# Rows parted by even and odd in a triangular inverse, element-wise work moved from GpSimd to VectorE, and gates one chunk ahead

## The chip, the cores and the metric

The kernel runs on one core of one Trainium2 chip. The metric is device time in microseconds (us) of one execution. The engines are TensorE (PE), VectorE (DVE), ScalarE (ACT), GpSimd (POOL) and SyncE (SP, which issues the DMAs here).

## The reference, cut to what matters

A first block (stick-breaking attention, cross-attention to a memory, a convolutional feed-forward) is followed by a second block, and the change touches the second alone. On 512 tokens of width 1024 it computes:

```python
h = rms_norm(x, pre_norm_w)
p = h @ w_in
p_rwkv, p_conv, p_pool, p_gate = split(p)
y_a = rwkv7_branch(...)    # 8 heads of 64; a linear recurrence over the 512 tokens
y_b = short_conv_branch(...)     # b * conv(c * u) * silu(z)
y_c = pool_branch(...)           # windows of 2, 4, 8, 16, mixed, * silu(z)
proj = einsum('nbsc,ncd->nbsd', stack([y_a, y_b, y_c]), w_branch)
gates = sigmoid(p_gate.reshape(b, s, 3, 1024))
merged = einsum('bsnd,nbsd->bsd', gates, proj)
out = x + rms_norm(merged @ w_out, post_norm_w)
```

The recurrence is computed in chunks of 64 tokens. Each chunk needs the inverse of a unit lower triangular 64x64 matrix, which is put together from the inverses of its two 32x32 diagonal blocks.

## The kernel before, in words

**Products and weights.** Everything is float32. A product is three passes of TensorE over a high and a low part of each operand (`mm3`: hi·hi, hi·lo, lo·hi). Weights come in units of 512 KB: SP loads `wr`, ACT casts it to `wh` (L135), and an engine subtracts for the low part `wl` (L136); which engine is what `lo_ring[0]` names, DVE as a rule, and GpSimd (`G`) while the inverse runs. Two units can be loaded ahead, four converted. A chunk is one unit's product with the whole input: 24 matmuls of 512 columns, into one of three PSUM banks of tag "g". The bank is free when DVE or ACT has read it. A product of a branch (`ps_br`) is 12 matmuls in a bank of the same three.

**Order.** Each engine runs its instructions in the order in which the program writes them. The program writes the chunks of the second block one after another: RWKV inputs, short convolution (`short_conv(i)`: four chunks each, read by `cu`, `cy`, `cz_s`), `merge(1)`, RWKV inputs, `pool(i)`, z chunks and `merge(2)`, gate chunks, `merge(0)`. Between them, `tick()`, once for about eight matmuls of 512 columns, moves generators on that run in the background. The table `WAIT` says for how many ticks each step of a generator waits. The RWKV branch is such a generator: `rwkv_steps(b)`, for b = 0 and 1, each for two of the four pairs of heads. Its first run lies beside `short_conv` and `merge(1)`, called the first stage here, its second beside the z chunks and `merge(2)`, the second stage.

**The inverse.** In `rwkv_steps` the 64 blocks of 32x32 lie in `ab`, one on each of 64 partitions. For j from 0 to 30, DVE multiplies a row of the block by a column of what is inverted so far (`tm`, L1142, (j+1)(31-j) elements a partition) and adds it to the rows not yet done (`xt`, L1144). After two values of j the generator yields for a tick. Then `xt` goes by a DMA to DRAM (`xtd`, L1151), comes back in another layout by four (`xc`, L1153), waits `WAIT["xc"]` ticks, is transposed on DVE (`xn`, L1157), and is multiplied on TensorE (`ps_x`, L1164), with the rest of the chunk solve, the states and the outputs behind it.

**The merges.** `merge(n)` goes through eight output slices d. For each it computes a gate chunk and its sigmoid (ACT, `gate`), then the branch product `ps_br` from the split branch output (`yb` for n = 1, `yp` for n = 2, L227 the high part on ACT, L228 the low part on GpSimd), and multiplies and adds on DVE and GpSimd (L1368 to L1371). Before the first `ps_br` the program ticks until all four parts of the branch output are split.

Of the kernel before, what the change touches and what calls it, by code (L numbers as in the profile page):

```python
# [10 lines left out]
F32 = mybir.dt.float32  # L11
# [39 lines left out]
class Split:  # L51
# [7 lines left out]
WAIT = {  # L59
# [5 lines left out]
}  # L65
# [3 lines left out]
def model_kernel(ctx: ExitStack, tc: tile.TileContext, a: dict, out: bass.AP, dbg: dict):  # L69
    nc = tc.nc  # L70
    stop = dbg.get("stop")
    V, G, A, T = nc.vector, nc.gpsimd, nc.scalar, nc.tensor
# [23 lines left out]
    def sub(s, *idx):  # L96
        return Split(s.hi[idx], s.lo[idx])
# [8 lines left out]
    ahead, lo_ring = [3], [V]  # L106
# [210 lines left out]
    for f0, f1 in parts:  # L317
# [6 lines left out]
        else:  # L324
# [1 line left out]
    units += [a["w_in"][16]]  # L326
    units += [a["w_in"][4 * n + p] for p in (0, 1) for n in range(3)]
    units += [a["w_in"][c + i] for i in range(4) for c in (21, 25, 17, 29)]
    merge_units = lambda n: [u for d in range(0, 8, 2)
                             for u in (a["w_in"][41 + 8 * n + d], a["w_br"][n, d // 2], a["w_in"][42 + 8 * n + d])]  # L330
    units += merge_units(1)
    units += [a["w_in"][4 * n + p] for p in (2, 3) for n in range(3)]
    units += [a["w_in"][c + i] for i in POOLS for c in (33, 37)]
# [209 lines left out]
    for hp in range(NPAIR):  # L543
# [6 lines left out]
        if hp:  # L550
            q = gemm_q()
            k = gemm_k()
        else:
# [6 lines left out]
            q, k = gemm_q(pss[0]), gemm_k(pss[1])  # L560
# [19 lines left out]
    for c in range(KC):  # L580
        ps = chunk(memT, M)
# [146 lines left out]
    for n in range(2):  # L728
# [7 lines left out]
        for m in range(2):  # L736
            d = (ALLS, m, slice(n * 512, (n + 1) * 512))
# [56 lines left out]
    for c in range(KC):  # L794
        ps = chunk(hT)
# [38 lines left out]
    x2 = dram.tile([NT, P, D], F32, name="x2")  # L834
# [33 lines left out]
    for pi, (f0, f1) in enumerate(parts):  # L868
        if pi:
            run_ahead(spare_in(bigt("wxh", [P, 8, 512]), bigt("wxl", [P, 8, 512])))  # L870
        for f in range(f0, f1):
# [3 lines left out]
            for isv in range(2):  # L875
                ps = lead.pop(0)() if lead else chunk(hT)
# [70 lines left out]
    b2 = ctx.enter_context(tc.tile_pool(name="b2", bufs=1))  # L947
# [4 lines left out]
    def temp(name, shape=None, dt=F32):  # L952
        return b2.tile(shape or [P, S], dt, tag="e", bufs=6, name=name)
# [4 lines left out]
    def quad(name, shape, dt=F32):  # L958
        return b2.tile(shape, dt, tag="q4", bufs=3, name=name)
# [25 lines left out]
    def silu(x, name, ps=False, make=temp):  # L985
        sg = make(name + "_s")
        A.activation(sg, x, AF.Sigmoid)
        (V if ps else G).tensor_tensor(sg, x, sg, ALU.mult)
        return sg

    NB2 = 2
# [6 lines left out]
    ycur, zss, ysplit, normed = {}, {}, set(), set()  # L998
# [7 lines left out]
    def rwkv_pair(p, ab, abd, a21):  # L1006

        r, k, v = rkv.pop(p)
        q = p % NB2
        sg, ai = slot("sg"), slot("ai")  # L1010
        for z, (o, b) in enumerate(((sg, "w0"), (ai, "a0"))):
            ps = bank("b", "ps_wa")
# [7 lines left out]
        ps = bank("b", "ps_ss")  # L1020
# [16 lines left out]
        ps = bank("b", "ps_ri")  # L1037
# [11 lines left out]
        ps = bank("b", "ps_rk")  # L1049
# [24 lines left out]
        ps = tokens(v)  # L1074
# [14 lines left out]
        for e in range(2):  # L1089
            for h in range(2):  # L1090
# [1 line left out]
                    nc.sync.dma_start(abd[q, e, :, h, c].rearrange("t j i -> j t i"),  # L1092
                                      aa[e][rows(2 * (1 - h) + c), h::2, 32 * c:32 * c + 32])
                nc.sync.dma_start(a21[rows(2 * h), q, 4 * e:4 * e + 4], aa[e][rows(2 * (1 - h)), h::2, 32:64])
        q0 = 32 * q
        nc.sync.dma_start(ab[q0:q0 + 32], abd[q].rearrange("e t h c j i -> (e t h c) j i"))
        yield wait["ac"]
        at_ = slot("at", [P, NT, P])
        A.copy(at_, tokens(ar[:, q, 0]))
# [2 lines left out]
        for h in range(2):  # L1102
            ps = tokens(kbh.rearrange("p t z i -> p (t z i)")[:, 512 * h:512 * h + 512])
# [3 lines left out]
        ps = bank("c", "ps_av", [P, NT, 2, CH])  # L1107
# [9 lines left out]
    def rwkv_steps(b):  # L1117

        pairs = (2 * b, 2 * b + 1)
        ab = quad("ab", [64, 32, 32])  # L1120
        abd = dram.tile([NB2, 2, NT, 2, 2, 32, 32], F32, name=f"abd{b}")
        xtd = dram.tile([NB2, 2, NT, 4, 32, 32], F32, name=f"xtd{b}")
        a21 = slot("a21", [P, NB2, 8, 32])
# [7 lines left out]

        yield from together(*[prepared(p) for p in pairs])

        xt = quad("xt", [64, 32, 32])
        G.memset(xt, 0.0)
        G.memset(xt.rearrange("p j i -> p (j i)")[:, 0::33], 1.0)
        yield
        lo_ring[0] = G
        for j in range(31):
            n = 31 - j  # L1140
            tm = b2.tile([64, 256], F32, tag="tm", bufs=1, name="tm")[:, 0:(j + 1) * n].rearrange("p (c i) -> p c i", i=n)
            V.tensor_tensor(tm, ab[:, j:j + 1, j + 1:32].to_broadcast([64, j + 1, n]),  # L1142
                            xt[:, 0:j + 1, j:j + 1].to_broadcast([64, j + 1, n]), ALU.mult)
            V.tensor_tensor(xt[:, 0:j + 1, j + 1:32], xt[:, 0:j + 1, j + 1:32], tm, ALU.add)  # L1144
            if j % wait["invn"] == wait["invn"] - 1:
                yield wait["inv"]
        lo_ring[0] = V

        xc = quad("xc", [P, 16, CH])
        G.memset(xc[:, :, 0:32], 0.0)  # L1150
        nc.sync.dma_start(xtd.rearrange("q e t c j i -> (q e t c) j i"), xt)  # L1151
        for c in range(4):
            nc.sync.dma_start(xc[rows(c), :, 32 * (c % 2):32 * (c % 2) + 32],  # L1153
                              xtd[:, :, :, c].rearrange("q e t j i -> j (q e t) i"))
# [12 lines left out]
        ps = blocks(a21.rearrange("p q n i -> p (q n) i"), xn, 0, 1)  # L1167
# [3 lines left out]
        ps = blocks(t1, xc[:, :, 32:64], 1, 0)  # L1171
# [113 lines left out]

    def y_split(i, x):
        yield wait["ysp"]
        split_to(x, ycur["t"][:, 0, i], ycur["t"][:, 1, i])
        ysplit.add(i)

    def rwkv_out(p):
# [7 lines left out]
    def short_conv(i):  # L1299
        ps = proj_in()  # L1300
        cu = temp("cu")
        A.copy(cu, ps)
        ps = proj_in()
        V.tensor_tensor(cu, ps, cu, ALU.mult)
        y = temp("cy")
        A.activation(y, cu, AF.Identity, scale=col("cw2", i))
        for r in (1, 0):
            V.scalar_tensor_tensor(y[:, 2 - r:S], cu[:, 0:S - 2 + r], col(f"cw{r}", i), y[:, 2 - r:S], ALU.mult, ALU.add)
        ps = proj_in()
        V.tensor_tensor(y, ps, y, ALU.mult)  # L1310
        zs = silu(proj_in(), "cz", ps=True)
        G.tensor_tensor(y, y, zs, ALU.mult)
        beside(y_split(i, y), 1)

    def pool(i, pw):
# [31 lines left out]
    def gate(g):  # L1347
        A.activation(g, proj_in(), AF.Sigmoid)
        return g

    def merge(n):
        if "t" not in mT:
            mT["t"] = bigt("merged", [P, KC, S], F32)
        merged = mT["t"]
        y = [sub(Split(ycur["t"][:, 0], ycur["t"][:, 1]), ALLS, i) for i in range(4)] if n else ya
        for d in range(KC):
            g = gate(temp("gate")) if n else gates[:, d]
            if d % 2 == 0:
                w = w_take()
            wv = Split(*[x.rearrange("p (c k n) -> p c k n", c=2, k=4) for x in (w.hi, w.lo)])  # L1360
            if n:
                until(lambda: len(ysplit) == 4)
            ps = bank("g", "ps_br")
            mm3(ps, [(sub(wv, ALLS, d % 2, k), y[k]) for k in range(4)])
            if d % 2:
                w_done()
            if n == 1:
                V.tensor_tensor(merged[:, d], ps, g, ALU.mult)  # L1368
            else:
                V.tensor_tensor(g, ps, g, ALU.mult)  # L1370
# [176 lines left out]
```

## Time and profile before

| | |
|---|---|
| median of 3 runs | 1387.27 us (1385.97 to 1388.68) |
| the profiled execution | 1386.43 us |
| its span in the profile | 1384.4 us |
| PE busy | 1334.0 us, 96% of the span |
| DVE, ACT, POOL busy | 842.1, 527.6, 343.6 us |
| mean granted TensorE clock | 0.99 |

The profiled execution is longer than its span by 2.0 us, which lie outside of what the profiler records. Times within the span count from its start. The first stage lies at about 915 to 975 us, the second at about 1155 to 1215 us.

### The profile page before, as it was taken

How to read it: one execution, taken by the hardware profiler on the slowest of the kernel's cores; microseconds unless marked ns; L12 is line 12 of the kernel's file. 1: busy time of each engine (PE TensorE's matmuls, PEld its weight loads, DVE VectorE, ACT ScalarE, POOL GpSimd, SP SyncE). 2: the span in 40 equal slices, each digit the busy share in tenths (PEclk: the TensorE clock that was granted, in tenths of full speed). 3: DMA queues.
4: the chain of work that ended last, by engine and by line, in shares of the span. 5: the costliest groups of instructions: out<-in, count | busy, mean ns of one | idle time of the engine just before them, and what ended most of it. 6: DMA issues, size and time to landing. Idle time of an engine off the chain costs nothing.

```text
span 1384.4 us, 19426 instructions
## 1 busy us (share of the span) xinstructions
PE 1334.0 (96%) x7780; PEld 1113.1 (80%) x7780; DVE 842.1 (61%) x1379; ACT 527.6 (38%) x780; POOL 343.6 (25%) x288
## 2 busy tenths in 40 slices
PE   8999999999999999999999989998999999999997
PEld 7888888778878888888888878786777777787876
DVE  5786887865576554522565766767335567734475
ACT  6565665134422534322343245332313543232330
POOL 1332432110002433400222332124001455311230
PEclk9999999999999999999999999999999999999999
DMA  5121343242223333232243132323222232222441
GB/s 186 63 84 53 97 154 123 88 141 92 76 76 109 120 98 101 91 107 91 92 137 107 48 106 76 104 84 91 63 77 92 69 90 82 82 72 77 134 140 61
DMA packets 50473, 132.71 MB, mean 96 GB/s; under 512 B 15440, under 2 KB 17360, under 8 KB 50384
## 3 DMA queue, kind: packets, MB, share of 16 engines
q1 hardware_dynamic: 50384, 131.48, 29.8%
q8 instruction: 61, 1.00, 0.3%
q14 instruction: 28, 0.23, 0.1%
HBM read 125.96 MB, written 5.24 MB: 95 GB/s over the span
## 4 chain that ended last, share of the span: by engine, by line
PE 73%; DVE 18%; ACT 4%; issue 3%; DMA 1%; POOL 1%; DVEq 0%; SPq 0%; POOLq 0%; ACTq 0%
PE ps_chunk L205 40%; PE ps_rows L205 9%; PE ps_d L205 6%; PE ps_v L205 4%; PE ps_lead L205 3%; DVE tm L1142 3%; PE ps_br L205 2%; DVE xt L1144 2%; DVE wl L136 2%; PE ps_o L517 1%; DVE lnt L626 1%; DVE rs_t L269 1%; PE ps_s L467 1%; PE ps_t L488 1%; PE ps_z L205 1%
## 5 line engine op out<-in xcount | busy, mean ns | idle before, releaser
L136 DVE TENSOR_TENSOR wl<-wr,wh 128x1024 fp32r<-128x1024 f32 x175 | 232.0, 1326 | 150.6 <-ACT wh L135 147.8
L135 ACT CAST wh<-wr 128x1024 fp32r<-128x1024 f32 x197 | 205.7, 1045 | 125.0 <-PE ps_d L205 51.2
L205 PE MATMUL ps_chunk<-h3Th,wh 128*128 128x512 f32 x488 | 128.3, 401 | 3.8 <-DVE gate L1370 2.1
L205 PE MATMUL ps_chunk<-h3Th,wl 128*128 128x512 f32 x488 | 127.4, 397 | 0.0
L205 PE MATMUL ps_chunk<-h3Tl,wh 128*128 128x512 f32 x488 | 125.6, 394 | 0.0
L850 DVE SCALAR_TENSOR_TENSOR c<-ps_chunk,colp,c 128x511 f32<-128x511 f32 x80 | 59.9, 749 | 90.4 <-ACT c L848 89.0
L205 PEld LDWEIGHTS ps_chunk<-h3Th,wh 128*128 128x128 f32 x488 | 92.1, 192 | 25.9 <-issue 6.1
L205 PEld LDWEIGHTS ps_chunk<-h3Tl,wh 128*128 128x128 f32 x488 | 90.2, 188 | 20.4 <-issue 1.5
L205 PEld LDWEIGHTS ps_chunk<-h3Th,wl 128*128 128x128 f32 x488 | 90.5, 189 | 19.0
L136 POOL TENSOR_TENSOR wl<-wr,wh 128x1024 fp32r<-128x1024 f32 x22 | 55.2, 2516 | 195.9 <-ACT wh L135 157.7
L856 POOL TENSOR_TENSOR c<-c 128x512 f32<-128x512 f32 x21 | 41.6, 1979 | 171.2 <-DVE c L850 151.1
L478 POOL TENSOR_TENSOR w<-r 128x511 f32<-128x511 f32 x40 | 58.7, 1468 | 85.5 <-DVE r L476 76.5
L205 PE MATMUL ps_chunk<-h2Th,wh 128*128 128x512 f32 x320 | 79.1, 389 | 0.0
L205 PE MATMUL ps_chunk<-h2Tl,wh 128*128 128x512 f32 x320 | 79.0, 389 | 0.0
L205 PE MATMUL ps_chunk<-h2Th,wl 128*128 128x512 f32 x320 | 79.0, 389 | 0.0
L848 ACT ACTIVATE c<-ps_chunk,colp 128x512 f32<-128x512 f32 x40 | 31.1, 778 | 111.7 <-PE ps_chunk L205 111.7
L205 PEld LDWEIGHTS ps_chunk<-h2Tl,wh 128*128 128x128 f32 x320 | 60.1, 188 | 12.4
L205 PEld LDWEIGHTS ps_chunk<-h2Th,wl 128*128 128x128 f32 x320 | 60.1, 188 | 12.4
L205 PEld LDWEIGHTS ps_chunk<-h2Th,wh 128*128 128x128 f32 x320 | 60.0, 188 | 12.4
L476 DVE TENSOR_TENSOR_SCAN r<-keep,masks 128x512 f32<-128x512 f32 x40 | 59.9, 1511 | 12.5 <-ACT keep L474 7.9
L205 PE MATMUL ps_chunk<-xTh,wh 128*128 128x512 f32 x128 | 35.5, 401 | 6.0 <-ACT xTh L357 6.0
L205 PE MATMUL ps_d<-wh,gvb 128*128 128x512 f32 x128 | 39.8, 389 | 0.0
(391 smaller groups left out, 2708.1 us busy)
## 6 DMA issues: line engine op xcount, KB each, us to landing
wr<-in_w_in_dram SPq DMA_DIRECT2D x65, 512.0 KB, 3.5
wr<-in_w_ff_dram SPq DMA_DIRECT2D x44, 512.0 KB, 3.6
wr<-in_w_dn_dram SPq DMA_DIRECT2D x22, 512.0 KB, 3.5
wr<-in_w_qk_dram SPq DMA_DIRECT2D x14, 512.0 KB, 3.5
wr<-in_w_br_dram SPq DMA_DIRECT2D x12, 512.0 KB, 3.6
wr<-in_w_v_dram SPq DMA_DIRECT2D x8, 512.0 KB, 3.6
wr<-in_w_xk_dram SPq DMA_DIRECT2D x8, 512.0 KB, 3.7
wr<-in_w_o_dram SPq DMA_DIRECT2D x8, 512.0 KB, 3.5
```

Source lines behind the costliest of these rows:

```text
L135: A.copy(w.hi, raw)
L136: lo_of.tensor_tensor(w.lo, raw, f32(w.hi), ALU.subtract)
L205: T.matmul(ps, l, r, start=start, stop=stop)
L269: V.scalar_tensor_tensor(t, y, nv, y, ALU.mult, ALU.mult)
L467: T.matmul(ps[:, o:o + n], q[e][:, tok(i)], part[:, 0:n], start=z == 0, stop=z == 1)
L476: V.tensor_tensor_scan(r[:, ::-1], keep[:, ::-1], masks[:, m, ::-1], 1.0, ALU.mult, ALU.max)
L478: G.tensor_tensor(t[:, 0:S - 1], r[:, 1:S], r[:, 0:S - 1], ALU.subtract)
L848: A.activation(c, ps, AF.Identity, scale=cw(2), bias=col("ffb", j))
L850: V.scalar_tensor_tensor(c[:, 2 - r:S], ps[:, 0:S - 2 + r], cw(r), c[:, 2 - r:S], ALU.mult, ALU.add)
L856: (V if end else G).tensor_tensor(cv, cg, cv, ALU.mult)
L1142: V.tensor_tensor(tm, ab[:, j:j + 1, j + 1:32].to_broadcast([64, j + 1, n]), xt[:, 0:j + 1, j:j + 1].to_broadcast([64, j + 1, n]), ALU.mult)
L1144: V.tensor_tensor(xt[:, 0:j + 1, j + 1:32], xt[:, 0:j + 1, j + 1:32], tm, ALU.add)
```

## The change

- `ab`, `tm` and `xt` use all 128 partitions: the even rows of `xt` lie on one half of the partitions and the odd rows on the other, so that a step handles j//2 + 1 rows of a partition, not j + 1. `ab` is loaded into both halves, and `xt` goes to DRAM as two DMAs of every second row.
- The low parts `wl` stay on DVE during the inverse. Also on DVE, and before on GpSimd: the multiplication of `silu`, the last product of `short_conv`, the low parts in `y_split`, and the additions of `merge(2)`.
- `merge(1)` and `merge(2)` compute gates one ahead of the branch products, with the units' order changed to suit.
- `WAIT["xc"]` is 14, before 10.

```diff
-    "pw2": 6, "pw3": 7, "mx": 4, "ysp": 1, "gl": 1, "xc": 10, "x1": 1, "x2": 2, "x3": 2, "so": 2, "mp": 2, "pp": 1,
+    "pw2": 6, "pw3": 7, "mx": 4, "ysp": 1, "gl": 1, "xc": 14, "x1": 1, "x2": 2, "x3": 2, "so": 2, "mp": 2, "pp": 1,
...
+    def merge_units(n):
+
+        us = [a["w_in"][41 + 8 * n]]
+        for d in range(8):
+            us += [a["w_in"][42 + 8 * n + d]] if d < 7 else []
+            us += [a["w_br"][n, d // 2]] if d % 2 == 0 else []
+        return us
...
-        (V if ps else G).tensor_tensor(sg, x, sg, ALU.mult)
+        V.tensor_tensor(sg, x, sg, ALU.mult)
...
+        for z in range(2):
+            q0 = 64 * z + 32 * q
+            nc.sync.dma_start(ab[q0:q0 + 32], abd[q].rearrange("e t h c j i -> (e t h c) j i"))
...
-        xt = quad("xt", [64, 32, 32])
+        xt = quad("xt", [P, 16, 32])
         G.memset(xt, 0.0)
...
-        lo_ring[0] = G
         for j in range(31):
-            n = 31 - j
...
+            n, m = 31 - j, j // 2 + 1
+            tm = b2.tile([P, 136], F32, tag="tm", bufs=1, name="tm")[:, 0:m * n].rearrange("p (c i) -> p c i", i=n)
+            V.tensor_tensor(tm, ab[:, j:j + 1, j + 1:32].to_broadcast([P, m, n]),
+                            xt[:, 0:m, j:j + 1].to_broadcast([P, m, n]), ALU.mult)
+            V.tensor_tensor(xt[:, 0:m, j + 1:32], xt[:, 0:m, j + 1:32], tm, ALU.add)
...
-        lo_ring[0] = V
...
-        nc.sync.dma_start(xtd.rearrange("q e t c j i -> (q e t c) j i"), xt)
+        for z in range(2):
+            nc.sync.dma_start(xtd.rearrange("q e t c j i -> (q e t c) j i")[:, z::2], xt[64 * z:64 * z + 64])
...
-        split_to(x, ycur["t"][:, 0, i], ycur["t"][:, 1, i])
+        split_to(x, ycur["t"][:, 0, i], ycur["t"][:, 1, i], V)
...
-        G.tensor_tensor(y, y, zs, ALU.mult)
+        V.tensor_tensor(y, y, zs, ALU.mult)
...
+        ahead_g = [gate(temp("gate"))] if n else []
         for d in range(KC):
-            g = gate(temp("gate")) if n else gates[:, d]
+            if n and d < KC - 1:
+                ahead_g.append(gate(temp("gate")))
+            g = ahead_g.pop(0) if n else gates[:, d]
...
-                G.tensor_tensor(merged[:, d], merged[:, d], g, ALU.add)
+                (V if n else G).tensor_tensor(merged[:, d], merged[:, d], g, ALU.add)
```

On DVE in the first stage, from the last quarter of `short_conv`, before: the sigmoid's product `cz_s`, and then nothing but inverse steps up to the next `cu`.

```order
L988 TENSOR_TENSOR cz_s<-ps_chunk,cz_s 128x512
L1142 TENSOR_TENSOR tm<-ab,xt 64x255
L1144 TENSOR_TENSOR xt<-xt,tm 64x17x15
L1142 TENSOR_TENSOR tm<-ab,xt 64x252
L1144 TENSOR_TENSOR xt<-xt,tm 64x18x14
L1142 TENSOR_TENSOR tm<-ab,xt 64x247
L1144 TENSOR_TENSOR xt<-xt,tm 64x19x13
```

In the changed kernel, at the same place (`cy` is the product with the sigmoid, `wl` a weight's low part, `yb` the low part of the branch output):

```order
L995 TENSOR_TENSOR cz_s<-ps_chunk,cz_s 128x512
L1320 TENSOR_TENSOR cy<-cy,cz_s 128x512
L1150 TENSOR_TENSOR tm<-ab,xt 128x135
L1152 TENSOR_TENSOR xt<-xt,tm 128x9x15
L1150 TENSOR_TENSOR tm<-ab,xt 128x126
L1152 TENSOR_TENSOR xt<-xt,tm 128x9x14
L136 TENSOR_TENSOR wl<-wr,wh 128x1024
L1150 TENSOR_TENSOR tm<-ab,xt 128x130
...
L1152 TENSOR_TENSOR xt<-xt,tm 128x11x10
L228 TENSOR_TENSOR yb<-cy,yb 128x512
```

The product, the weight's low part and `yb` now stand between the steps of the inverse, whose steps have half the elements.

On PE at the first branch product of the first stage, before: one gate chunk (the three rows ahead of `ps_br`), then `ps_br`, and `ps_x` of the RWKV branch in the next gate chunk.

```order
L205 MATMUL ps_chunk<-h3Th,wl 128x512 x8
L205 MATMUL ps_br<-yb,wh 128x512 x8
L205 MATMUL ps_br<-yb,wl 128x512 x4
L205 MATMUL ps_chunk<-h3Th,wh 128x512 x8
L205 MATMUL ps_chunk<-h3Tl,wh 128x512 x8
L1164 MATMUL ps_x<-xn,a_7042 32x32 x32
```

Now, from the same chunk on:

```order
L205 MATMUL ps_chunk<-h3Th,wl 128x512 x8
L205 MATMUL ps_chunk<-h3Th,wh 128x512 x8
L205 MATMUL ps_chunk<-h3Tl,wh 128x512 x8
L205 MATMUL ps_chunk<-h3Th,wl 128x512 x8
L205 MATMUL ps_br<-yb,wh 128x512 x8
L205 MATMUL ps_br<-yb,wl 128x512 x4
L205 MATMUL ps_chunk<-h3Th,wh 128x512 x8
L205 MATMUL ps_chunk<-h3Tl,wh 128x512 x8
L205 MATMUL ps_chunk<-h3Th,wl 128x512 x8
L1172 MATMUL ps_x<-xn,a_7042 32x32 x32
```

The first branch product stands one gate chunk later, and the first `ps_x` 32 matmuls of 512 columns later.

On SP the store of the inverse and the reads behind it, before:

```order
L114 DMA wr<-in_w_in_dram 128x1024 x2
L1151 DMA xtd_7041<-xt 64x1024
L1153 DMA xc<-xtd_7041 32x16x32 x4
L114 DMA wr<-in_w_br_dram 128x1024
L114 DMA wr<-in_w_in_dram 128x1024 x2
```

Now:

```order
L114 DMA wr<-in_w_in_dram 128x1024
L1159 DMA xtd_7041<-xt 1024x1x32 x2
L1161 DMA xc<-xtd_7041 32x16x32 x4
L114 DMA wr<-in_w_in_dram 128x1024
L114 DMA wr<-in_w_br_dram 128x1024
```

One store of 64 rows of 1024 elements has become two of 1024 rows of 32.

## Rows read from the trace of the kernel before

**Rows 1.** The page, part 1: busy time of each engine, its share, its instructions.

```profile
PE 1334.0 (96%) x7780; PEld 1113.1 (80%) x7780; DVE 842.1 (61%) x1379; ACT 527.6 (38%) x780; POOL 343.6 (25%) x288
```

**Rows 2.** Windows: stretch; length; busy PE, PEld, DVE, ACT, POOL; clock; DMA.

```profile
915.40:957.50 42.10, 40.37 (x177) 32.78 (x175) 38.49 (x72) 9.41 (x12) 16.45 (x8) 1.00 0.22 64
1155.20:1198.00 42.80, 38.12 (x153) 30.31 (x152) 40.88 (x70) 11.27 (x15) 22.25 (x13) 0.92 0.18 55
960.00:965.00 5.00, 3.09 (x7) 2.44 (x8) 1.57 (x1) 1.80 (x3) 4.27 (x4) 0.51 0.48 73
```

**Rows 3.** PE timeline, first stage: start, length, instruction; idle before, releaser.

```profile
946.26 1.98 PE L205 MATMUL ps_chunk<-h3Tl,wh 128*128 128x512 f32 x8
948.07 1.98 PE L205 MATMUL ps_chunk<-h3Th,wl 128*128 128x512 f32 x8
951.74 2.09 PE L205 MATMUL ps_chunk<-h3Th,wh 128*128 128x512 f32 x8 [1.69 <-DVE cu L1304]
...
958.27 0.94 PE L205 MATMUL ps_br<-yb,wh 128*128 128x512 f32 x3 [0.81 <-DVE cy L1310]
961.91 2.50 PE L205 MATMUL ps_br<-yb,wh 128*128 128x512 f32 x5 [2.70 <-ACT yb L227]
...
971.11 1.20 PE L1164 MATMUL ps_x<-xn,a 32*32 32x32 f32 x64 [0.91 <-issue]
```

**Rows 4.** PE timeline, second stage.

```profile
1163.35 1.98 PE L205 MATMUL ps_chunk<-h3Th,wl 128*128 128x512 f32 x8
1166.79 1.20 PE L205 MATMUL ps_br<-yp,wh 128*128 128x512 f32 x4 [1.47 <-ACT yp L227]
1169.06 2.07 PE L205 MATMUL ps_br<-yp,wh 128*128 128x512 f32 x4 [1.08 <-POOL yp L228]
...
1181.98 1.98 PE L205 MATMUL ps_chunk<-h3Th,wh 128*128 128x512 f32 x8
...
1189.24 1.07 PE L205 MATMUL ps_br<-yp,wl 128*128 128x512 f32 x4
1192.44 2.08 PE L205 MATMUL ps_chunk<-h3Th,wh 128*128 128x512 f32 x8 [2.14 <-DVE gate L1370]
```

**Rows 5.** DVE timeline, first stage: two products `tm` of one size, the last step.

```profile
932.23 0.41 DVE L1142 TENSOR_TENSOR tm<-ab,xt 64x252 f32<-64x252 f32 x1
...
937.29 2.52 DVE L1142 TENSOR_TENSOR tm<-ab,xt 64x252 f32<-64x252 f32 x1
...
957.33 0.20 DVE L1144 TENSOR_TENSOR xt<-xt,tm 64x31 f32<-64x31 f32 x1
```

**Rows 6.** POOL timeline beside it.

```profile
936.94 2.59 POOL L136 TENSOR_TENSOR wl<-wr,wh 128x1024 fp32r<-128x1024 f32 x1
```

**Rows 7.** DVE groups by line: first stage (two rows), second stage (two rows).

```profile
L1142 DVE TENSOR_TENSOR tm<-ab,xt 64x31 f32<-64x31 f32 (+15 forms) x31 | 21.0, 678 | 0.9
L1144 DVE TENSOR_TENSOR xt<-xt,tm 64x31 f32<-64x31 f32 (+15 forms) x31 | 12.3, 398 | 1.1
...
L1144 DVE TENSOR_TENSOR xt<-xt,tm 64x31 f32<-64x31 f32 (+15 forms) x31 | 20.5, 662 | 1.1
L1142 DVE TENSOR_TENSOR tm<-ab,xt 64x31 f32<-64x31 f32 (+15 forms) x31 | 16.9, 546 | 0.9
```

**Rows 8.** DVE timeline, ops of the sizes that move, with GpSimd idle.

```profile
847.29 0.69 DVE L228 TENSOR_TENSOR rkl<-rk,rkh 128x512 fp32r<-128x512 f32 x1 [0.69 <-ACT rkh L227]
...
894.75 1.22 DVE L136 TENSOR_TENSOR wl<-wr,wh 128x1024 fp32r<-128x1024 f32 x1
```

**Rows 9.** DMA issues: queue, count, KB of one, median us from issue to landing.

```profile
abd<-aa SPq DMA_DIRECT2D x32, 16.0 KB, 1.7
...
xtd<-xt SPq DMA_DIRECT2D x2, 256.0 KB, 3.2
xc<-xtd SPq DMA_DIRECT2D x8, 64.0 KB, 2.1
```

**Rows 10.** SP timeline, the reads behind the store.

```profile
961.10 1.94 SPq L1153 DMA_DIRECT2D xc<-xtd  x4
```

More of the change, by code (lines that the diff above doesn't have):

```diff
@@ L328, in model_kernel @@
     units += [a["w_in"][c + i] for i in range(4) for c in (21, 25, 17, 29)]
-    merge_units = lambda n: [u for d in range(0, 8, 2)
-                             for u in (a["w_in"][41 + 8 * n + d], a["w_br"][n, d // 2], a["w_in"][42 + 8 * n + d])]
+    def merge_units(n):
[4 more added lines that the diff above has]
+        return us
     units += merge_units(1)
@@ L1094, in rwkv_pair @@
                 nc.sync.dma_start(a21[rows(2 * h), q, 4 * e:4 * e + 4], aa[e][rows(2 * (1 - h)), h::2, 32:64])
-        q0 = 32 * q
-        nc.sync.dma_start(ab[q0:q0 + 32], abd[q].rearrange("e t h c j i -> (e t h c) j i"))
+        for z in range(2):
+            q0 = 64 * z + 32 * q
+            nc.sync.dma_start(ab[q0:q0 + 32], abd[q].rearrange("e t h c j i -> (e t h c) j i"))
         yield wait["ac"]
@@ L1119, in rwkv_steps @@
         pairs = (2 * b, 2 * b + 1)
-        ab = quad("ab", [64, 32, 32])
+        ab = quad("ab", [P, 32, 32])
         abd = dram.tile([NB2, 2, NT, 2, 2, 32, 32], F32, name=f"abd{b}")
@@ L1132, in rwkv_steps @@
         yield from together(*[prepared(p) for p in pairs])
-        xt = quad("xt", [64, 32, 32])
+        xt = quad("xt", [P, 16, 32])
         G.memset(xt, 0.0)
-        G.memset(xt.rearrange("p j i -> p (j i)")[:, 0::33], 1.0)
+        for z in range(2):
+            G.memset(xt[64 * z:64 * z + 64].rearrange("p j i -> p (j i)")[:, z::34], 1.0)
         yield
-        lo_ring[0] = G
         for j in range(31):
-            n = 31 - j
[L1141 to L1144, printed above, removed]
+            n, m = 31 - j, j // 2 + 1
[3 more added lines that the diff above has]
+            V.tensor_tensor(xt[:, 0:m, j + 1:32], xt[:, 0:m, j + 1:32], tm, ALU.add)
             if j % wait["invn"] == wait["invn"] - 1:
                 yield wait["inv"]
-        lo_ring[0] = V
         xc = quad("xc", [P, 16, CH])
         G.memset(xc[:, :, 0:32], 0.0)
-        nc.sync.dma_start(xtd.rearrange("q e t c j i -> (q e t c) j i"), xt)
+        for z in range(2):
+            nc.sync.dma_start(xtd.rearrange("q e t c j i -> (q e t c) j i")[:, z::2], xt[64 * z:64 * z + 64])
         for c in range(4):
```

## The prediction

> **What bounds the kernel now.** The busy times come first: PE is busy 96% of the span [rows 1], so a change beside it can only give back PE's idle time and time at the lower clock. I then read PE's timeline through the second block and looked where the starts are further apart than the work. At full clock eight matmuls of 512 columns start 1.81 us apart (946.26 to 948.07, [rows 3]), 0.2266 each. That gives the loss of a stretch: its length less its matmuls times 0.2266.
>
> First stage [rows 3]: from 948.07 to 971.11 there are 23.04 us and 60 such matmuls (8, 24 of the chunk at 951.74, 12 of `ps_br`, 16 of the next chunk), 13.60 us of work; **9.44 us are lost**. Idle: 1.69 and 0.81 on DVE's `cu` and `cy`, 2.70 on ACT's `yb`, 0.91 at `ps_x`, 6.1 in all. The rest is clock: after those waits the window from 960 to 965 shows 0.51 [rows 2], the 1.2 GHz level for nearly all of it. Second stage [rows 4]: from 1163.35 to 1181.98 are 18.63 us with 56 matmuls, 12.69 of work; 5.94 lost, of which 1.47 and 1.08 are waits for the two parts of `yp`. From 1189.24 to 1192.44 are 3.20 us with 4 matmuls, 0.91; 2.29 lost on a gate product `gate` L1370. **Together 8.2 us.** The two stages hold 17.7 us that no work of PE needs.
>
> What is late there is DVE. In the two windows around the inverse it is busy 38.49 of 42.10 and 40.88 of 42.80 us [rows 2], and `cu`, `cy` and the gate product stand behind the inverse steps in its order. At 957.33 it begins the last step of an inverse [rows 5] that stands, in the program, 16 matmuls ahead of PE's 948.07, so at 944.5: 13 us behind. But much of that busy time isn't work. One and the same product `tm` of 64x252 took 0.41 us at 932.23 and 2.52 at 937.29 [rows 5], and the second lies beside GpSimd's `wl`, 936.94 for 2.59 [rows 6]. The step of 64x31 took 0.20. From 0.41 and 0.20 the unblocked price is 0.17 + 0.00095 per element. Over 62 operations and 2 x 5456 elements this makes 20.9 us; measured were 33.3 in the first stage and 37.4 in the second [rows 7]. **12.4 and 16.5 us are blocking by GpSimd.**
>
> The Trainium skill states this as a rule ("SBUF — State Buffer", section "SBUF: two separate sides"): VectorE and GpSimd share a port pair under an exclusive lock, which a VectorE operation with two SBUF inputs needs against a GpSimd operation that reads SBUF, and the loser fully blocks. The pair 0.41 and 2.52 agrees.
>
> **The change part by part.**
>
> The halved inverse: the number of elements falls from 5456 to 2856 for products and additions each (the sum of (j//2+1)(31-j)); 62 x 0.17 + 5712 x 0.00095 = 16.0 us, 4.9 less a stage.
>
> The moves to DVE: in the first window five `wl` (1.22 alone, [rows 8]), one `cy` product and one `yb` part (0.69 each, by the row of 128x512) come to DVE, 7.5 us. Its sum: 38.5 - 12.4 - 4.9 + 7.5 = 28.7 us, with 2 to 3 of waits for ACT's casts in between about 31. PE gives the inverse 16 ticks of 1.81, 29.0. DVE ends 2 to 3 us behind the program, not 13. In the second window five `wl`, two `z_s`, one `yp` and two additions of `merged` come: 6.1 + 5 x 0.69 = 9.6; 40.9 - 16.5 - 4.9 + 9.6 = 29.1, up to 32 because two `yal` splits stay on GpSimd and may still block. PE's own work there is 42.8 - 8.2 = 34.6. So DVE keeps up in both. Bounds: if nothing of the blocking came back, the first window's sum would be 41.1, as full as now.
>
> Gates ahead: the first `ps_br` stands one more gate chunk, 24 x 0.2266 = 5.44 us, later. First stage: the last chunk of `short_conv` ends at 949.9 and `ps_br` is due at 949.9 + 10.9 = 960.8. Between lie sigmoid, two products, a cast and the low part, five operations at about 0.7, a `wl`, and the lag of 2 to 3: ready at about 957 to 958, some 3 us ahead. Second stage: `yp` was late by 1.47 + 1.08 = 2.55; even if it came no sooner, 5.44 cover it. A gate product now has the 12 matmuls of the next `ps_br` and a chunk less the bank's reuse; I put its slack at about 2 us. If this cover were gone, the waits of [rows 3, 4] return at their price.
>
> The wait of 14: the whole solve starts 4 ticks later, `ps_x` 32 matmuls, 7.25 us. I cost it at nothing: the chunks of `merge` and of the inputs behind it cover the solve, and in the changed program's order the last output of the RWKV branch stands at the same place ahead of `merge(0)` as before. Without that cover it would cost the 7.25 in the second stage.
>
> The store and loads: `ab` by two DMAs more in a stage hides before the inverse. The store of `xt` becomes 2048 pieces of 128 B, which no row shows. From below: four reads `xc` of 512 pieces each, 2048 pieces in all, are issued within 1.94 us [rows 10] and land in 2.1 [rows 9], so all within about 3.6 us; the old store took 3.2. From above: `abd`, 128 such pieces in 1.7 us [rows 9], all of it by the piece: 27 us. I take 3.6, the row with as many pieces. It is hidden as long as it ends within the wait: the last step is let go at 944.5 and `ps_x` due at 948.07 + (60 + 32) x 0.2266 = 968.9; these 24.4 us less the lag 2.6, the reads 3.6 and the transpose 0.7 leave 17.5; a weight unit that lands behind `xc` on SP's queue and is cast ahead of a gate's sigmoid comes due 3 us sooner, 14.6.
>
> What is late next: in the run of RWKV outputs beside `merge(1)`, one or two operations of 0.69 more stand on DVE ahead of a normalization that PE waits for: between 0 and 1.4, I take 0.6. And at the tight places of the second stage (slack 1 to 2) a `wl` can come in between: half of 1.22 at two places, 1.2, with bounds of 0 and 5.8 (two thirds of the second stage's loss back).
>
> The sum, against the profiled execution, 1386.43, of which the span is 1384.4 (the median shown is 0.84 above it): 1386.4 - 9.4 - 8.2 + 0.6 + 1.2 = **1370.5 us**, with 1367 to 1374.5 as this case's own range.
>
> **The rivals.**
>
> One place fails (1374.5 to 1381): DVE, in order, now waits for ACT's casts and sigmoids itself where GpSimd waited before, and one of the four waits returns with its low clock. For it: idle of DVE behind ACT was GpSimd's to bear before. Against: slacks of 2 to 3 us. One place is worth 2.3 (gate) to 9.4 (first stage); with 4 to 10 it is about 1378.
>
> DVE becomes the bound (1384 to 1390): moved work fills it. For it speaks its busy share in [rows 2], 91 and 96%. If blocked time weren't given back, the sum would be 41.1 us against 29.0 of PE's ticks: the 17.7 stay. Against: the pair in [rows 5], and that blocking needs a GpSimd operation beside it, of which five or more per stage go.
>
> By the Trainium skill ("Trainium Kernel Development and Optimization", section "Best Practices", item 5) the occupancy of an engine other than TensorE is fine as a measure; by that the move onto an engine 91% busy would gain nothing, the second rival's 1387. The rows of one operation with two durations say otherwise.
>
> The store is late (slower): its 128 B pieces go by the price of `abd`. It decides from 14.6 us a stage; at 27 it costs 12.6 in each, 1370.5 + 25.2 = 1396. The time is over 1389 from about 24 us for the store on. For it: `abd`'s price by the piece. Against: `xc`'s 2048 pieces in 3.6.
>
> The Trainium skill ("DMA: Bandwidth & Descriptors", sections "Specifications" and "Why small descriptors are slow (HBM only)") speaks for this rival: under 512 B a transfer isn't at line rate, and each packet has a fixed overhead. The reads of 128 B show little of it.
>
> **How the numbers follow.** A measurement of this kernel tells about 0.2%, 2.8 us, from no change. Both stages clean 0.64; better than 1367, if more lags behind DVE elsewhere goes too, 0.02; one place fails 0.20; DVE bound 0.09, of which 0.07 within 0.2% and 0.01 each beyond; store late 0.05. Faster 0.02 + 0.64 + 0.20 + 0.01 = 0.87, same 0.07, slower 0.06. The range from 1366 to 1381 holds the first and third case and leaves out 0.16.
>
> **What would show it.** No operation of the inverse over 0.4 us beside a GpSimd operation (its two groups at 15 to 18 us a stage); PE without idle ahead of the first `ps_br` of either merge and a granted clock of 1.00 there; the inverse's last step 8 to 10 us earlier against PE's chunks; the new store landing within 4 to 6 us. It would be wrong if the groups stay above 25 us, if `ps_br` waits for DVE's `yb` or `yp`, or if `ps_x` waits for `xn`.

## The result, and the profile after

The changed kernel takes a median of **1369.94 us**, before 1387.29; the ratio is 0.9866, with an interval from 0.9853 to 0.9879, 1.2 to 1.5% faster. The forecast was 1370.5. The profile below is of a later run of the same kernel (median 1369.56, ratio 0.9869 [0.9854, 0.9884], profiled execution 1369.36, span 1367.5), because the first one was taken at a low granted clock (mean 0.655) from end to end.

The page's busy times of the changed kernel, beside [rows 1]:

```profile
PE 1327.1 (97%) x7780; PEld 1110.0 (81%) x7780; DVE 831.1 (61%) x1413; ACT 527.7 (39%) x780; POOL 284.6 (21%) x256
```

PE is busy 6.9 us less, DVE 11.0 us less though it took over work, POOL 59 us less. The windows between the first and the last step of the inverse in both stages, that around the first branch product of `merge(1)`, and one between the stages (columns as in [rows 2]):

```profile
915.10:946.10 31.00, 31.00 (x138) 25.72 (x137) 27.44 (x79) 9.02 (x11) 0.00 (x0) 1.00 0.26 85
1148.20:1179.00 30.80, 30.80 (x138) 25.46 (x137) 28.18 (x77) 10.11 (x15) 3.07 (x3) 1.00 0.20 69
955.00:965.00 10.00, 10.00 (x46) 8.29 (x45) 3.69 (x4) 3.19 (x4) 0.82 (x1) 1.00 0.49 162
...
1100.00:1105.00 5.00, 5.00 (x15) 3.97 (x16) 4.33 (x7) 2.05 (x3) 3.65 (x5) 0.67 0.08 17
```

Before, the inverse filled 42.1 and 42.8 us; now 31.0 and 30.8, with PE busy throughout at a clock of 1.00. Around the first `ps_br` the clock is 1.00, before 0.51. What fell is the two groups of the inverse, first stage ahead of second, against [rows 7]:

```profile
L1152 DVE TENSOR_TENSOR xt<-xt,tm 128x126 f32<-128x126 f32 (+22 forms) x31 | 7.9, 256 | 1.1
L1150 DVE TENSOR_TENSOR tm<-ab,xt 128x126 f32<-128x126 f32 (+22 forms) x31 | 7.9, 253 | 0.7
...
L1152 DVE TENSOR_TENSOR xt<-xt,tm 128x126 f32<-128x126 f32 (+22 forms) x31 | 10.0, 323 | 1.1
L1150 DVE TENSOR_TENSOR tm<-ab,xt 128x126 f32<-128x126 f32 (+22 forms) x31 | 7.9, 254 | 0.8
```

15.8 and 17.9 us, before 33.3 and 37.4. PE's timeline at the places of [rows 3] and [rows 4]:

```profile
947.73 1.98 PE L205 MATMUL ps_chunk<-h3Th,wl 128*128 128x512 f32 x8
949.54 1.98 PE L205 MATMUL ps_chunk<-h3Th,wh 128*128 128x512 f32 x8
...
958.61 1.98 PE L205 MATMUL ps_chunk<-h3Th,wl 128*128 128x512 f32 x8
960.42 1.98 PE L205 MATMUL ps_br<-yb,wh 128*128 128x512 f32 x8
...
1160.40 1.98 PE L205 MATMUL ps_chunk<-h3Th,wl 128*128 128x512 f32 x8
1162.21 1.98 PE L205 MATMUL ps_br<-yp,wh 128*128 128x512 f32 x8
...
1188.50 1.07 PE L205 MATMUL ps_br<-yp,wl 128*128 128x512 f32 x4
1189.41 1.98 PE L205 MATMUL ps_chunk<-h3Th,wh 128*128 128x512 f32 x8
...
1200.38 1.20 PE L1172 MATMUL ps_x<-xn,a 32*32 32x32 f32 x64
```

No row has a wait at its end. The chunk at 947.73 is the one that began at 948.07 before; `ps_br` starts 1.81 us behind its predecessor's start, as if nothing had to come from another engine. DVE at the inverse's end and at the two parts that `ps_br` needs:

```profile
945.90 0.19 DVE L1152 TENSOR_TENSOR xt<-xt,tm 128x16 f32<-128x16 f32 x1
...
952.84 1.53 DVE L228 TENSOR_TENSOR yb<-cy,yb 128x512 fp32r<-128x512 f32 x1
...
1158.06 1.40 DVE L1152 TENSOR_TENSOR xt<-xt,tm 128x115 f32<-128x115 f32 x1
...
1159.99 0.68 DVE L228 TENSOR_TENSOR yp<-pz_s,yp 128x512 fp32r<-128x512 f32 x1
```

The last step starts at 945.90. In the program it stands 16 matmuls ahead of 947.73, so at 944.1: DVE is 1.8 us behind, before 13. The step of 1.40 us at 1158.06 is one of two in the second stage that lie beside a `yal` split still on GpSimd.

What is left between the stages, first in the changed kernel and then before:

```profile
1045.22 0.65 PE L1282 MATMUL ps_yT<-ident,misc 128*128 128x128 f32 x4 [0.84 <-POOL misc L1277]
...
1080.04 0.50 PE L1058 MATMUL ps_rk<-rkh,bd1r 128*128 128x512 f32 x1 [2.44 <-ACT sg L1021]
...
1098.15 0.46 PE L1091 MATMUL ps_ac<-misc,kb 64*128 64x128 f32 x2 [1.43 <-DVE arr L1095]
...
1107.52 0.39 PE L1058 MATMUL ps_rk<-rkh,bd1r 128*128 128x512 f32 x1
```

```profile
1089.28 0.50 PE L1051 MATMUL ps_rk<-rkh,bd1r 128*128 128x512 f32 x1 [2.71 <-ACT sg L1014]
...
1107.46 0.46 PE L1084 MATMUL ps_ac<-misc,kb 64*128 64x128 f32 x2
...
1115.22 0.39 PE L1051 MATMUL ps_rk<-rkh,bd1r 128*128 128x512 f32 x1
```

`ps_rk` waits as before (2.44, before 2.71); `ps_yT` now waits 0.84 and `ps_ac` 1.43, with a window at 0.67 behind it. From the first `ps_rk` shown to the last are 27.48 us, before 25.94: 1.5 us were lost again between the stages.

### The profile page after: what moved, and what is told of

The parts are those of the page before. It is cut to its first block, busy times and chain, and to the rows that moved or that the text cites. A ratio compares the mean times of both kernels' runs of the same rounds, so it can differ in the third digit from the quotient of the medians.

```text
span 1869.7 us, 19424 instructions
## 1 busy us (share of the span) xinstructions
PE 1854.7 (99%) x7780; PEld 1279.4 (68%) x7780; DVE 821.0 (44%) x1413; ACT 530.7 (28%) x780; POOL 274.6 (15%) x256
## 4 chain that ended last, share of the span: by engine, by line
PE 99%; DVE 0%; DMA 0%; ACT 0%; DVEq 0%; issue 0%; SPq 0%; ACTq 0%
PE ps_chunk L205 54%; PE ps_rows L205 13%; PE ps_d L205 6%; PE ps_br L205 5%; PE ps_v L205 5%; PE ps_lead L205 3%; PE ps_s L474 1%; PE ps_o L524 1%; PE ps_t L495 1%; PE ps_o L205 1%; PE ps_z L205 1%; PE ps_hT L645 1%; PE ps_ac L1091 1%; PE ps_w L1194 1%; PE ps_tok L1078 1%; PE ps_y L1258 0%
## 5 line engine op out<-in xcount | busy, mean ns | idle before, releaser
L136 DVE TENSOR_TENSOR wl<-wr,wh 128x1024 fp32r<-128x1024 f32 x185 | 243.1, 1314 | 202.0 <-ACT wh L135 201.6
L205 PE MATMUL ps_chunk<-h3Th,wl 128*128 128x512 f32 x488 | 175.3, 512 | 0.0
L205 PE MATMUL ps_chunk<-h3Th,wh 128*128 128x512 f32 x488 | 174.2, 508 | 0.0
L205 PE MATMUL ps_chunk<-h3Tl,wh 128*128 128x512 f32 x488 | 173.4, 508 | 0.0
L205 PEld LDWEIGHTS ps_chunk<-h3Th,wl 128*128 128x128 f32 x488 | 100.7, 209 | 53.2 <-issue 16.5
L205 PE MATMUL ps_chunk<-h2Th,wl 128*128 128x512 f32 x320 | 112.5, 504 | 0.0
L205 PE MATMUL ps_chunk<-h2Th,wh 128*128 128x512 f32 x320 | 111.6, 509 | 0.0
L205 PE MATMUL ps_chunk<-h2Tl,wh 128*128 128x512 f32 x320 | 111.1, 508 | 0.0
L205 PEld LDWEIGHTS ps_chunk<-h2Tl,wh 128*128 128x128 f32 x320 | 66.1, 207 | 38.6 <-issue 13.9
L136 POOL TENSOR_TENSOR wl<-wr,wh 128x1024 fp32r<-128x1024 f32 x12 | 29.0, 2426 | 244.9 <-ACT wh L135 244.9
L205 PE MATMUL ps_d<-wh,gvb 128*128 128x512 f32 x128 | 53.7, 508 | 0.0
L205 PE MATMUL ps_chunk<-xTh,wh 128*128 128x512 f32 x128 | 47.6, 511 | 5.6 <-ACT xTh L364 5.6
```

The lines of the kernel that those rows point to most:

```text
L136: lo_of.tensor_tensor(w.lo, raw, f32(w.hi), ALU.subtract)
L205: T.matmul(ps, l, r, start=start, stop=stop)
```

## The experiments

The change has three parts: the halved inverse (H), the moves to VectorE (M), and the gates ahead with the longer wait (G). Six kernels have one or two of them. Times are medians, with the ratio to the kernel before in the same set of runs; an interval is about 0.0015 to either side.

| parts | time, us | ratio | gain by the ratio, us |
|---|---|---|---|
| H | 1382.77 | 0.9951 | 6.8 |
| M | 1381.10 | 0.9944 | 7.8 |
| G | 1383.17 | 0.9959 | 5.7 |
| H, M | 1375.54 | 0.9904 | 13.3 |
| H, G | 1374.65 | 0.9904 | 13.3 |
| M, G | 1373.99 | 0.9900 | 13.9 |
| H, M, G | 1369.56 | 0.9869 | 18.2 |

The single parts add up to 20.3, the whole is 18.2: the gains nearly add, and the pairs (14.6, 12.5 and 13.5 by their singles) agree within the intervals. (The expectation of H below names pair gains of 13.2, 13.9 and 14.2 us; by the ratios they are those of the table.)

**The whole change once more.** No edit; its profile is the one above.

> The changed kernel once more, for a profile at the full clock. If the two stages lost their idle time as predicted: median within 1368 to 1372 us; the two groups of the inverse at 15 to 18 us a stage; no idle ahead of the first ps_br of either merge; the new store landed within 4 to 6 us. If the gain has another source: the groups above 25 us a stage, or waits ahead of ps_br still there.

All of the first alternative was seen, with the second stage's groups (17.9) at the upper end. Of the waits between the stages it said nothing.

**H and M, without the gates ahead.**

```diff
-    ... "xc": 14, ...
+    ... "xc": 10, ...
-        ahead_g = [gate(temp("gate"))] if n else []
...
+            g = gate(temp("gate")) if n else gates[:, d]
```

> The change without the gates ahead and with the wait at 10: halved inverse and moves to VectorE alone. Theory A (the blocking of VectorE by GpSimd is most of the loss): most of the gain stays, 1371 to 1377 us, with one short wait ahead of the first ps_br of merge(2), about 1 to 2.5 us, since yp comes no sooner. Theory B (the gates ahead hide a VectorE that is late anyway): 1380 us or more, with the waits for yb and yp back at 3 to 4 us.

1375.54 us, theory A. The waits on PE's timeline in the two stages:

```profile
964.33 1.20 PE L1166 MATMUL ps_x<-xn,a 32*32 32x32 f32 x64 [1.05 <-issue]
...
1159.01 1.21 PE L205 MATMUL ps_br<-yp,wh 128*128 128x512 f32 x4 [0.48 <-ACT yp L227]
1162.29 1.81 PE L205 MATMUL ps_br<-yp,wh 128*128 128x512 f32 x4 [2.07 <-DVE yp L228]
```

In the first stage the first `ps_br` doesn't wait even without the gates ahead: there VectorE alone was late. In the second the two parts of `yp` are late by 0.48 and 2.07, 2.55 in all. [rows 4] has the same sum with GpSimd doing the low part, but that is chance: the shares differ, and the sum is 1.92 with H alone and 3.51 with M alone. In every kernel without the gates ahead PE waits here, whichever engine does the low part; with them it waits only beside the multiplications further below.

**H and G, GpSimd keeps its work.**

```diff
+        lo_ring[0] = G
         for j in range(31):
...
-        V.tensor_tensor(y, y, zs, ALU.mult)
+        G.tensor_tensor(y, y, zs, ALU.mult)
```

and likewise for `silu`, `y_split` and the additions.

> The change without the moves: halved inverse and gates ahead, GpSimd keeps its work beside the inverse. Theory A: the blocking stays, the two groups of the inverse take 24 to 30 us a stage, a part of the loss is back, 1374 to 1380 us. Theory C (the number of elements and the order were the point, the blocking isn't): 1369 to 1372 us, groups at 16 to 18 us.

1374.65 us, theory A; the groups are 28.4 and 32.0 us, the second above its 24 to 30. First stage, second stage, and the wait that came of it:

```profile
L1151 DVE TENSOR_TENSOR tm<-ab,xt 128x126 f32<-128x126 f32 (+22 forms) x31 | 18.5, 598 | 0.9
L1153 DVE TENSOR_TENSOR xt<-xt,tm 128x126 f32<-128x126 f32 (+22 forms) x31 | 9.9, 318 | 1.1
...
L1153 DVE TENSOR_TENSOR xt<-xt,tm 128x126 f32<-128x126 f32 (+22 forms) x31 | 16.2, 521 | 1.1
L1151 DVE TENSOR_TENSOR tm<-ab,xt 128x126 f32<-128x126 f32 (+22 forms) x31 | 15.8, 508 | 0.9
```

```profile
1177.97 2.11 PE L205 MATMUL ps_chunk<-h3Th,wh 128*128 128x512 f32 x8 [2.80 <-DVE gate L1384]
```

Half the elements, and still 12.6 and 14.1 us more than with the moves. Blocking hardly depended on how long the VectorE operations were.

**M and G, the old inverse.**

```diff
-        xt = quad("xt", [P, 16, 32])
+        xt = quad("xt", [64, 32, 32])
```

with `ab`, `tm`, the steps and the store as before.

> The change without the halving: the old inverse on 64 partitions, moves and gates ahead. By the sum VectorE has 33.6 us of work and 2 to 3 of waits against 29 of ticks in the first stage, and ends 7 us late; the gate ahead covers 5.4 of it. Theory A: groups at 20 to 23 us a stage, 1370 to 1375 us. Theory C (halving is the point): 1378 us or more.

1373.99 us, theory A. Groups of 20.7 and 22.8 us: the unblocked old inverse, which the prediction put at 20.9. PE no longer waits in the first stage; in the second it does:

```profile
1190.13 2.11 PE L205 MATMUL ps_chunk<-h3Th,wh 128*128 128x512 f32 x8 [0.87 <-DVE gate L1378]
...
1203.81 1.53 PE L1169 MATMUL ps_x<-xn,a 32*32 32x32 f32 x64 [2.49 <-issue]
```

The second wait isn't for the reads `xc`, issued at 1187.81 and landed 2 to 2.5 us later. `ps_x` needs `xn`, which VectorE began at 1203.00, right behind other work in its order; ahead of that stands a `wl` that had waited 2.15 us for ACT's cast, and the cast 2.88 us for its weight's DMA. The weights stand on SP behind the store and the reads, which came late with the inverse; that the lateness came this way is read from the order, not tried.

**The parts alone.**

> The halved inverse alone; GpSimd keeps its work, no gates ahead, wait of 10. If the gains of the parts add (the three kernels with two parts each gained 13.2, 13.9 and 14.2 us, all three parts about 19), the halving alone is worth about 6.5 us: 1381 to 1383. If one part alone already takes VectorE out of the way, 1376 to 1378; if the halving only helps together with another, 1386 or more. Groups of the inverse at 27 to 33 us a stage, since GpSimd still blocks.

> The moves to VectorE alone; old inverse, no gates ahead, wait of 10. If the gains add, 1380 to 1383 us; groups of the inverse at 20 to 23 us a stage, and VectorE about 6 us late, so that the waits for yb and yp stay in part, 1 to 3 us each. If VectorE becomes the bound without the halving (the second rival), 1386 or more.

> The gates ahead and the wait of 14 alone; old inverse, GpSimd keeps its work. If the gains add, 1379 to 1382 us: the 5.4 us of the gate chunk cover yp's 2.6 in the second stage and part of the first, but the waits for cu and for a gate product stay, which come from VectorE. If the cover is all that is wanted, 1372 to 1375; groups of the inverse at 33 to 38 us, as before.

H alone took 1382.77 and M alone 1381.10, as expected of gains that add. The groups were 28.5 and 32.7 us with H alone, 21.5 and 23.5 with M alone. With M alone PE waited 1.18 us for `yb`, as expected, and 1.14 and 2.37 for the parts of `yp`, more than the 1 to 3. G alone took 1383.17, 1.2 more than expected. Its rows tell why:

```profile
951.68 2.08 PE L205 MATMUL ps_chunk<-h3Th,wh 128*128 128x512 f32 x8 [1.70 <-DVE cu L1312]
...
958.21 2.08 PE L205 MATMUL ps_chunk<-h3Th,wh 128*128 128x512 f32 x8 [0.83 <-DVE cy L1318]
...
1183.75 3.78 PE L205 MATMUL ps_chunk<-h3Th,wh 128*128 128x512 f32 x8 [6.47 <-DVE gate L1381]
```

The waits of [rows 3] for `cu` and `cy` are there again (1.70 and 0.83), since no gate helps there; both waits for `yp` are gone, but PE runs on into a PSUM bank that VectorE, blocked, hasn't read: 6.47 us, where [rows 4] had 2.14. The cover alone moved the stall to where the late engine is next waited for. The expectation had the wait for the gate product stay, not grow.

**The wait of 14.** The whole change but for one number:

```diff
-    ... "xc": 14, ...
+    ... "xc": 10, ...
```

> The whole change but for the wait, which is 10 again. xn then comes due 7.25 us sooner, at about 957 where the reads end at about 955 in the first stage: a wait of 0 to 2 us ahead of ps_x in each. 1368 to 1373 us; if the later solve costs something downstream (the stall at ps_ac, 1.43 us, which the kernel before has not), that goes and the time is 1368 or less; if not, ps_ac keeps its stall and the time is that of the changed kernel or up to 3 us more.

1369.34 us, ratio 0.9858 [0.9845, 0.9872]: no difference that can be told from the change. `ps_ac` and `ps_yT` didn't wait in it, and `ps_x` did in the second stage:

```profile
1193.36 1.20 PE L1172 MATMUL ps_x<-xn,a 32*32 32x32 f32 x64 [0.96 <-issue]
```

Neither alternative of the expectation held: the stall at `ps_ac` went, and the time didn't fall with it. What took its place is shown further below, under "Why `ps_ac` waits".

**GpSimd's work against GpSimd's reads.** Two kernels have scratch work on GpSimd ahead of the loop over j, on top of the change: 40 multiplications, or 60 fills.

```diff
+        for _ in range(40):
+            G.tensor_tensor(gsc, gsc, gsc, ALU.mult)
...
+        for _ in range(60):
+            G.memset(gsc, 1.0)
```

> The changed kernel with 40 multiplications of a scratch tile of 128x160 added on GpSimd (output used by nothing), written right ahead of the inverse of each stage, so that they run beside its first part. If GpSimd's access to SBUF blocks VectorE, a step beside them waits for up to one of them: 0.2 to 0.5 us more for each of about 20 to 40 steps, groups of the inverse at 25 to 35 us a stage, 15.8 and 17.9 without. If the long steps came of something else (the weights' subtraction itself, its DMA), the groups stay within 1 us.

> The changed kernel with 60 fills (memset) of the same scratch tile of 128x160 on GpSimd in the same place: GpSimd is busy, but reads nothing in SBUF. If only GpSimd operations that read SBUF block VectorE's steps, the groups of the inverse stay at 15.8 and 17.9 us within 1 us a stage; if any GpSimd operation blocks, they grow as with the multiplications.

In the first stage GpSimd was done with either before the inverse began (with the multiplications at 914.2, and the first step at 916.4), and the groups were 15.7 us in both kernels; that stage tests nothing. In the second stage they ran beside it. The multiplications, and the groups in the second stage:

```profile
1147.71 25.26 POOL L1150 TENSOR_TENSOR gsc<-gsc 128x160 f32<-128x160 f32 x40
```

```profile
L1154 DVE TENSOR_TENSOR tm<-ab,xt 128x126 f32<-128x126 f32 (+22 forms) x31 | 12.5, 404 | 0.8
L1156 DVE TENSOR_TENSOR xt<-xt,tm 128x126 f32<-128x126 f32 (+22 forms) x31 | 11.5, 372 | 1.1
```

The fills, and the groups:

```profile
1146.75 17.31 POOL L1150 MEMSET gsc<- 128x160 f32 x60
```

```profile
L1154 DVE TENSOR_TENSOR tm<-ab,xt 128x126 f32<-128x126 f32 (+22 forms) x31 | 9.0, 289 | 0.8
L1156 DVE TENSOR_TENSOR xt<-xt,tm 128x126 f32<-128x126 f32 (+22 forms) x31 | 8.9, 287 | 1.1
```

Beside 25.3 us of multiplications the groups took 24.0 us, 6.1 more; beside 17.3 us of fills 17.9, no more than without. 24.0 is a little under the range expected. One step of one size beside the multiplications, and beside the fills:

```profile
1153.34 0.50 DVE L1154 TENSOR_TENSOR tm<-ab,xt 128x56 f32<-128x56 f32 x1
```

```profile
1151.04 0.22 DVE L1154 TENSOR_TENSOR tm<-ab,xt 128x56 f32<-128x56 f32 x1
```

Most steps beside the multiplications took about 0.50 us, 0.2 to 0.3 more than without, near the lower end of what was expected for a step. Many short operations blocked less than a few long ones: in the first stage before, 16.5 us of GpSimd's work [rows 2] cost 12.4. Each of the two kernels has one run. The one with the multiplications took 1381.03 us, that with the fills 1370.56, and in the first PE waited as it had before the change:

```profile
1165.99 1.19 PE L205 MATMUL ps_br<-yp,wh 128*128 128x512 f32 x4 [1.41 <-DVE yp L228]
...
1181.97 3.36 PE L205 MATMUL ps_chunk<-h3Th,wh 128*128 128x512 f32 x7 [5.72 <-DVE gate L1385]
```

So the long steps don't come from the weights' subtraction as such, nor from GpSimd's being busy. The multiplications read SBUF and the fills read nothing; that the reading makes the difference fits this. A GpSimd operation that reads and computes nothing was not tried.

**A version past both.** The split of the pool's weights (`pw`) is cast on ACT when its DMA lands, ahead of the sigmoid `sg` that `ps_rk` waits for. Here it is done 5 ticks later by a generator, and `WAIT["ye"]` is 5, before 4; the second version has 4 there, and `WAIT["xc"]` 12.

```diff
-    pw = split_to(pw_raw, pw[:, 0], pw[:, 1])
+    pw = Split(pw[:, 0], pw[:, 1])
+    def pw_split():
+        yield
+        split_to(pw_raw, pw.hi, pw.lo)
+    beside(pw_split(), 5)
```

> The changed kernel with the split of the pool weights (pw) moved 5 ticks later, out of ACT's way ahead of the sigmoid that ps_rk waits for, and the wait ahead of ps_yT 5, not 4. If the two stalls between the stages are the waits that they look like, the 2.44 us at ps_rk and the 0.84 at ps_yT go, with the low clock behind: 1365 to 1367 us. If what PE gains there is lost at ps_ac again (1.43 us and its clock), 1368 to 1370.

> The changed kernel with the split of pw 5 ticks later and the wait of the inverse's reads 12, between 10 (which showed no stall at ps_yT or ps_ac but 0.96 us at ps_x of the second stage) and 14. If those stalls hang on how the generator falls against the chunks, 1364 to 1367 us and no idle over 1 us between 900 and 1300 us; otherwise as the kernel with 14, 1365 to 1370.

1365.93 us, ratio 0.9843 [0.9828, 0.9859], all five runs (1364.19 to 1367.04) below the fastest of the change, 1368.58; and 1366.42, 0.9848 [0.9832, 0.9864]. These are runs of another set than the change's, and the interval of the first version's ratio overlaps a little with the change's, which begins at 0.9854. `ps_rk` no longer waits, and `ps_yT` only 0.23 us in the second. `ps_ac` does, 1.95 us in the first and 1.93 in the second, so that the first expectation held for the time though the stall at `ps_ac` came too, and the second for the time and not for "no idle over 1 us":

```profile
1075.81 0.40 PE L1058 MATMUL ps_rk<-rkh,bd1r 128*128 128x512 f32 x1
...
1094.30 0.46 PE L1091 MATMUL ps_ac<-misc,kb 64*128 64x128 f32 x2 [1.95 <-DVE arr L1095]
```

## Why the prediction was right, point by point

**What bounds.** The 17.7 us of idle time and low clock in the two stages were given back in whole: no row of either stage waits in the changed kernel. In spans of PE's timeline: from a `ps_av` ahead of the first stage (911.50 before, 911.15 after) to the `ps_rk` that waits (1089.28, 1080.04) are 168.9 us, before 177.8; from a `ps_av` ahead of the second (1151.20, 1142.82) to a branch product of `merge(0)` (1328.23, 1311.24) 168.4, before 177.0. So the first gave back 8.9 us, after the new 0.84 at `ps_yT`, and the second 8.6, where the sum had 9.4 and 8.2 without it. That much of VectorE's busy time was blocking by GpSimd is shown three ways: the groups with and without the moves (28.4 against 15.8 us at the same number of elements), the old inverse at 20.7 us without GpSimd beside it (20.9 in the prediction), and the multiplications that bring blocking back where fills don't. The last also fits the second half of the rule in the Trainium skill ("SBUF — State Buffer", section "SBUF: two separate sides"), by which it takes a GpSimd operation that reads SBUF: 24.0 us against 17.9. Blocking isn't all of the lateness: in the sum the moves take 12.4 us of it off the first stage and put 7.5 of work on, 4.9 net, as much as the halving, and H alone gained nearly as much as M alone (6.8 and 7.8 us).

**The halved inverse**: 16.0 us predicted, 15.8 measured in the first stage, 17.9 in the second, where two steps took about 1 us too much each beside the `yal` splits; the sum had up to 2.9 for them.

**The moves**: a sum of 28.7 us in the first window, 27.4 busy measured, and of 29.1 to 32 in the second, 28.2 measured; lag 2 to 3 predicted, 1.8 measured. The rival by which VectorE becomes the bound is refuted, also without the halving: M alone gains 7.8 us. The Trainium skill's remark that occupancy is a fine measure of the distance to roofline for engines other than TensorE ("Trainium Kernel Development and Optimization", section "Best Practices", item 5) led the wrong way here: of the 91% busy a third was blocking, and VectorE is still 89% busy in a window that is 11 us shorter.

**Gates ahead**: `yb` was ready at 954.4 for 960.4, 6 us early where 3 were predicted; `yp` at 1160.7 for 1162.2. In the second stage the cover is needed, as the sum said: without it the 2.55 us of waits are there. At `ps_br` in the first it is worth nothing.

**The wait of 14** was costed at nothing, and the run with 10 agrees in its time. In parts it isn't nothing: with 10 `ps_x` waits 0.96 us, and with 14 `ps_yT` waits 0.84.

**The store**: 3.6 us taken for its 2048 pieces; the two DMAs of half the size land 4.3 us after their issue, and issuing both took SP 1.30 us. From the store's issue to that of the reads behind it are 5.0 us in the first stage (946.21 to 951.22), before 3.5, so the term was too small, and hidden. The rival of a late store, from 14.6 us on, is refuted; the piece price of `abd` doesn't scale. The store in the changed kernel, columns as in [rows 9]:

```profile
xtd<-xt SPq DMA_DIRECT2D x4, 128.0 KB, 4.3
```

**The rest of the sum.** `ps_yT`: 0.6 taken, 0.84 measured, but not for the reason given, the operations moved to VectorE. It waited 0.82 to 0.84 us in every kernel with `xc` at 14 and `ye` at 4, also in G alone and in H with G, where nothing is moved; 0.23 in the one with 12, and not at all with 10. So it is the longer wait, costed at nothing, that makes it, and the size came out by luck. The 1.2 us for tight places of the second stage were **misplaced**: nothing was lost there. The stretch between the stages lost 1.5 us up to the last `ps_rk` shown and won 0.7 back before the next `ps_av`, a place that the prediction didn't look at. The total is right in part because these two are of one size. The terms of the sum add up to 1370.6; against the profiled execution the forecast is 1.1 us too high, and some 0.3 of the shorter span lies outside of the stretches named here.

**The signs.** Two came out otherwise than named: two steps of the second stage lie beside a GpSimd operation and took 1.40 and 1.27 us, not under 0.4, and the last step of the first stage came 11 us earlier against PE's chunks, not 8 to 10.

**Why `ps_ac` waits** in the change and not before. In the trace it waits for DVE's `arr`, and no one part of the change makes it: it waited 1.4 to 2 us in all kernels with the wait of 14, but also in two with 10 (H, and H with M) and in the one with 12, and not in M alone nor in the whole change with 10. The granted clock tells them apart. The window behind the first `ps_rk` before the change, in the changed kernel, and with the wait of 10 (columns as in [rows 2]):

```profile
1090.00:1095.00 5.00, 5.00 (x21) 4.16 (x20) 4.17 (x10) 1.00 (x2) 1.55 (x1) 0.68 0.24 92
```

```profile
1080.00:1085.00 5.00, 4.96 (x26) 4.22 (x27) 4.81 (x7) 1.76 (x3) 1.87 (x2) 1.00 0.31 105
```

```profile
1080.00:1085.00 5.00, 4.84 (x19) 4.04 (x20) 4.24 (x6) 1.88 (x4) 1.87 (x2) 0.67 0.35 105
```

In the 2.5 us behind `ps_rk` the clock is 0.50 to 0.60 in the three kernels where `ps_ac` doesn't wait (before, M alone, and the change with 10), and 1.00 in all where it does. `arr` comes no later: it starts 17.62 us after `ps_rk` before the change and 17.55 in it. PE at full clock is there first. So either the clock or the wait costs PE its time here, and the run with 10 gains nothing by having no wait.

**What stays open.** Why the clock falls behind `ps_rk` in some kernels and not in others: PE idled 2.6 to 2.9 us ahead of it in the three where it fell, and up to 2.8 in those where it didn't.

## What to carry to other kernels

Before an engine's busy share is taken as work, look for one operation of one shape with two durations, and at what lies beside the longer one: here a third of VectorE's busy time beside the inverse was blocking by GpSimd, and the "full" engine finished sooner for taking over GpSimd's work. A cover (work put between a late producer and its consumer) helped here only against the producer that it stood behind; the late engine was met again at the next bank that it had to read. When a stall goes, the next one is where the same chain is tight for another reason, so look at the stretches between the stages too.

## What the runs showed of the hardware that was not expected

Blocking depended on the GpSimd operations more than on VectorE's: halving VectorE's elements left the blocked time as it was, 12.6 and 16.2 us over the unblocked 15.8 with GpSimd's work in place, before 12.4 and 16.5. And fills on GpSimd, 17.3 us of them beside the inverse, cost VectorE nothing that the groups show (17.9 against 17.9 us).
